# Moving the first third of the second layer's modulation product from between the layers to ahead of the first layer's routing

## The chip, the core and the metric

The kernel is one program on one core of a Trainium2 chip. TensorE does the matrix products, VectorE, ScalarE and GpSimd the rest; SyncE starts most of the transfers. The metric is the device time of one execution in microseconds (us), less being better. Times of day in this text are us from the start of the profiled execution's span.

## The reference

A block of two layers works on 256 latent and 256 context tokens of width 1024. Each layer modulates and normalizes the stream, mixes tokens, and adds a mixture of 16 experts, of which each token uses two. Cut to what matters here:

```
for layer in range(2):
    mod_l = cond_lat @ ada_w[layer] + ada_b[layer]          # ada_w: [2, 1024, 6144]
    mod_c = cond_ctx @ ada_w[layer] + ada_b[layer]
    sh1, sc1, g1, sh2, sc2, g2 = split(mod, 6)               # for latent and for context tokens
    n = rms_norm(h, norm_mix_g[layer]) * (1 + sc1) + sh1
    m = mixer(n)                                             # layer 0: convolution and scan; layer 1: convolution and attention
    h = h + g1 * (m @ w_out[layer])
    h = h + moe(rms_norm(h, norm_ffn_g[layer]) * (1 + sc2) + sh2)
out = rms_norm(h_lat, final_g)

def moe(t):
    score = sigmoid(t @ router_w)
    sel = (score + router_bias).reshape(-1, 4, 4)            # best group by its two best experts,
    ...                                                      # then the two best experts in it
    for e in range(16):
        out += combine[:, e] * ((silu(t @ w_gate[e]) * (t @ w_up[e])) @ w_down[e])
```

The change is about the columns `sh1, sc1` of `mod` in layer 1: the first 2048 of the 6144 columns of `ada_w[1]`, 8 MB. They depend on the conditioning vector alone, so they can be worked out at any time before the second layer's first normalization.

## The kernel before

**Precision.** Weights are split into a high half (`hi`, cast on ScalarE, L138) and the rest (`lo`, subtracted on VectorE, L140), and each product is three fast matmuls of halves. Such a pair of tiles is called `hl`. The modulation matrix is not split: it is multiplied as plain float32.

**The weight ring.** One object, `feed`, reads weight units of 1 MB ([128, 2048] float32) by transfers started from SyncE's queue into a ring of buffers: 3 called `raw`, 7 `rawx`, and 1 `rawy` that comes with the experts. `feed.one()` splits half a unit; after the second half of a unit `feed.load()` starts the next load into a buffer that is free. A load into a buffer whose splits aren't done waits on SyncE, and all that stands behind it in SyncE's program waits too. Before the experts, `moe()` sets `feed.gate = one`: the scale of the `hi` casts is then the tile `one`, which VectorE writes at the end of the routing (L1196), so that the splits of the first expert's weights come behind the routing.

**Layer 0, in order of time.** Output projection of the mixer (L788); routing; experts; the second layer's normalization `norm_T(1)` (L472 to L490); projections of the second mixer (L456). Tokens are in four tiles of 128.

**Routing.** Four tiles `H` give logits (L839) and, on VectorE and GpSimd, the normalized tokens `xn` (`normed`, L854 to L861), which SyncE writes to the DRAM table `XN` in four transfers of 512 KB (L861). `route()` ranks the scores on VectorE (L1082, then L998 to L1097), TensorE counts with a triangular matrix (`tri`, L1101), and VectorE makes the lists `dispi` (L1133), with which GpSimd gathers the first expert's tokens from `XN` into `xg` (L1134). `xg` is zeroed before on ScalarE (L1169). TensorE turns `xg` (L1150) and the first expert starts (L1162). Between routing and experts each engine reads the largest load `cnti` and jumps over a branch (L1007, L1008) that handles experts with over 128 tokens and isn't taken here.

**The moved product.** `Ada(1, 0)` covers the 2048 columns in eight units of 1 MB, each 256 columns wide, in rows of 1 KB (`ada_unit`, L330). One step (`channel_vectors`) is 8 float32 matmuls (L428), a copy on ScalarE (L430), and `channel_finish`: 2 small matmuls (L437) and one or two additions on VectorE (L441, L445) into the vectors `SH` and `SC`. In the kernel before, steps are made two at a time ahead of the columns k = 0, 2, 4, 6 of `norm_T(1)`, whose own work is 4 float32 matmuls for each k (L480), scale and shift by `SC`, `SH` on VectorE (L485) and ScalarE (L487), and a split (L489, L490). The loads are started in the tail of layer 0, three of them beside the reads of the experts' sums `YD`.

**What sets the order.** A scheduler at build time puts the instructions of each engine in one fixed row; the rows shown below under the change are read from the built programs. Engines run their rows in that order and wait by semaphores.

Of the kernel before, what the change touches and what calls it, by code (L numbers as in the profile page):

```python
# [17 lines left out]
NE = 16  # L18
# [29 lines left out]
HOLD = 0  # L48
ADA_PRE = 3
# [13 lines left out]
class Feeder:  # L63


    def __init__(self, tc, pool):
        self.tc, self.nc, self.pool = tc, tc.nc, pool
        self.boost = BOOST
        self.todo, self.loaded, self.ready = deque(), deque(), deque()
        self.extra, self.n, self.ahead, self.only = None, 0, 3, False  # L70
        self.gate = self.extra2 = self.hl = None
        self.np, self.part = 0, []
        self.ada, self.na, self.ns, self.pool_lo = None, 0, 0, 0

    def add(self, src, inner, columns=False):

# [19 lines left out]

    def load(self, n=99):
        limit = self.slots() if self.extra else 2
        while self.todo and len(self.loaded) < limit and n:
            n -= 1  # L100
            src, inner, columns = self.todo.popleft()
            t = self.raw_tile(True)
            if self.gate is not None:
                self.nc.vector.tensor_copy(t[:, 0:1], self.last)
            dst = t.rearrange("p (k f) -> p k f", f=inner)
            if callable(src):
                src = src()
            if type(src) is tuple:
                for i, part in enumerate(src):
                    self.nc.sync.dma_start(dst[:, :, 128 * i:128 * i + 128], part)  # L110
            else:
                self.nc.sync.dma_start(dst, src)
            self.loaded.append((t, columns))
# [55 lines left out]
def _body(tc, nc, pool, psum, dram, a):  # L169
# [39 lines left out]
    feed = Feeder(tc, pool)  # L209
# [297 lines left out]
    cmL, PL = open_pool("mix0_left")  # L507
# [234 lines left out]
    def add_experts(layer, u0, u1):  # L742
        parts = [("up", 0)]
        for e in range(NE):
            parts += [("gate", e)] + [("up", e + 1)] * (e + 1 < NE) + [("down", e)]
        us = []
        for part, e in parts:
            w = a["moe_w_" + part][layer, e].rearrange("(p k) f -> p k f", p=128)
            step = 2 if part == "down" else 4
            us += [(w[:, k0:k0 + step], 2048 // step) for k0 in (0, step)]  # L750
        for u in us[u0:u1]:
            feed.add(*u)
# [60 lines left out]
    ada_fill(40)  # L813
    feed.ada = None
    close_pool(cmR)
    add_experts(0, 0, 6 * NE - HOLD)
    cmX, PX = open_pool("raw0", "right")
    feed.extra, feed.n = (PX, RAWB0), -1
    feed.pool_lo = 0
# [249 lines left out]
    def route(layer, nt):  # L1069

        n_ = nt

        def xsteps(n):
            for st in XSTEPS[nt][n].split():
                normed(layer, int(st[0]), int(st[1]))

        xsteps(0)
        ins = S.activation(score[:, :nt], selt[:, :nt], AF.Sigmoid)
        mark("router", ins)
        dump(f"score{layer}", score)  # L1080
        se, sc = selt[:, :n_], score[:, :n_]
        V.tensor_tensor(se, sc, RB.unsqueeze(1).broadcast_to([128, n_, NE]), OP.add)  # L1082
        se4 = se.rearrange("p t (g e) -> p (t g) e", g=4)
        rk = rank[:, :n_]
        rk4 = rk.rearrange("p t (g e) -> p (t g) e", g=4)
        ranks(rk4, se4, 4 * n_)
        mk = mask[:, :n_]
        mk4 = mk.rearrange("p t (g e) -> p (t g) e", g=4)
        V.tensor_scalar(mk, rk, 1.5, None, OP.is_lt)
        xsteps(1)  # L1090
        pt_ = posm[:, :n_]
        V.tensor_tensor(pt_, mk, se, OP.mult)
        V.tensor_reduce(gsc[:, :n_].rearrange("p t g -> p (t g)"), pt_.rearrange("p t (g e) -> p (t g) e", g=4), AX.X, OP.add)
        ranks(grk[:, :n_], gsc[:, :n_], n_)
        V.tensor_scalar(grk[:, :n_], grk[:, :n_], 0.5, None, OP.is_lt)
        V.tensor_tensor(mk4, mk4, grk[:, :n_].rearrange("p t g -> p (t g)").unsqueeze(2).broadcast_to([128, 4 * n_, 4]), OP.mult)
        V.tensor_copy(maskb[:, :n_], mk)  # L1097

        pp_ = bank()
        for i in range(n_):  # L1100
            T.matmul(pp_[:, NE * i:NE * i + NE], tri, maskb[:, i], start=True, stop=i == 0)  # L1101
            for i2 in range(i):
                T.matmul(pp_[:, NE * i:NE * i + NE], oneb, maskb[:, i2], start=False, stop=i2 == i - 1)

        V.tensor_scalar(rk, rk, 0.5, pcol[:, 1:2], OP.is_gt, OP.add)
        if layer == 0:
            V.tensor_copy(RM[:, :n_, :, 0], rk)
        V.tensor_scalar(mk, mk, -16384.0, 16384.0, OP.mult, OP.add)
        V.tensor_tensor(posm[:, :n_], mk, pp_[:, :NE * n_].rearrange("p (t e) -> p t e", t=n_), OP.add)
        return xsteps, se, sc, mk, rk  # L1110

    def moe(layer, nt, pl, before_tail=None):
        A = Am[layer]
        n_ = nt
        xgs = [pl.tile([128, D], F32, name="xg", tag="xg", bufs=2) for _ in range(2)]

        xsteps, se, sc, mk, rk = route(layer, nt)

        def slots(e):
# [181 lines left out]
        with in_order():  # L1301
            expert(NE - 2)
            yss = [feed.raw_tile(True) for _ in range(nt)]
            for i in range(nt):
                Q.dma_start(yss[i], YD[256 * i:256 * i + 256].rearrange("(p t) d -> p (t d)", t=2))
            if before_tail:
                before_tail()
            for r in range(nt // 2):
                for nh in range(2):
                    S.activation(gbs[r][:, 512 * nh:512 * nh + 512], row_bc(A, 2, 2, r, nh), AF.Copy)  # L1310

            def add(i, st):
                ys = yss[i]
                if st == 0:
                    G.tensor_tensor(ys[:, :D], ys[:, :D], ys[:, D:], OP.add)
                elif st == 1:
                    V.tensor_tensor(ys[:, :D], ys[:, :D], gbs[i // 2], OP.mult)
                else:
                    V.tensor_tensor(Hi(i), Hi(i), ys[:, :D], OP.add)

            for i in range(nt):
                add(i, 0)
            for i in range(nt):
                for st in (1, 2):
                    later.append(lambda i=i, st=st: add(i, st))
            expert(NE - 1)
# [405 lines left out]
        for h in range(2):  # L1732
            feed.add(cdw[:, :, col0 + 256 * h:col0 + 256 * h + 256], 256, True)

    ada10 = Ada(1, 0)

    def prepare_mixer1():
        feed.only = True
        ada10.load(ADA_PRE)
        feed.only = False  # L1740

    def mixer1_weights():
        cblk(2048)
        cblk(1536)
# [6 lines left out]
                feed.add(w1[:, 4 * kh:4 * kh + 4, 512 * nh:512 * nh + 512], 512)  # L1751

    cmL, PL = open_pool("moe0")
    moe(0, 4, PL, prepare_mixer1)
    close_pool(cmL)
    close_pool(cmY)
    feed.extra2 = None
    feed.only = True
    ada10.load(3 - len(ada10.q))
    dump_h("H0")  # L1760
    if dbg.get("stop") == 1:
        return
# [2 lines left out]
    pend.extend(Ada(l, t) for l, t in ((0, 1), (0, 2), (1, 0), (1, 1), (1, 2))[3:])  # L1765
    cmM, PM = open_pool("mix1_m")
    cmL, PL = open_pool("mix1_n")
    nT = norm_T(1, PL, ada10)
    feed.extra, feed.only = None, False
    mixer1_weights()  # L1770
    feed.load()
    close_pool(cmX)
# [239 lines left out]
```

## Time and profile before

| what | value |
|---|---|
| median of 3 runs | 1205.16 us (1202.92 to 1210.82) |
| the profiled execution | 1208.15 us, its span 1206.5 us |
[...]
| TensorE busy | 1074.3 us, 89% |
| VectorE busy | 857.6 us, 71% |
| ScalarE busy | 716.6 us, 59% |
| GpSimd busy | 274.2 us, 23% |
| moved by DMA | 320.91 MB, mean 266 GB/s |

The profiled execution took 2.99 us more than the median, and 1.65 us of it lie outside its span. TensorE is the engine with the most work, so time is to be won where it stands still. The two stretches that the change touches are short: the routing of layer 0 (about 278 to 302) and the step from layer 0 to layer 1 (about 626 to 663).

### The profile page before, as it was taken

The page shows a single profiled execution, that of the slowest core. Times are in us where ns is not written, and L with a number is a line of the kernel's source. Part 1 is how long each engine was busy: PE and PEld are TensorE (multiplying, and loading weights), DVE is VectorE, ACT ScalarE, POOL GpSimd, SP SyncE. Part 2 cuts the span into 40 slices and gives each one's busy share as a digit, 9 for nine tenths or more (in the row PEclk, how much of TensorE's full clock was granted, in tenths as well). Part 3 has the DMA queues.
Part 4 walks back from the last instruction along what each step waited for, and adds up shares of the span by engine and source line. Part 5 has one row for each costly group of instructions (what it writes and reads, how often), then busy time and mean ns, then how long its engine had stood idle before and what let it go on. Part 6 is the DMA issues. An engine that isn't in the chain of part 4 may idle for free. (4 is left out here: it accounts for less than half of the span.)

```text
span 1206.5 us, 15581 instructions
## 1 busy us (share of the span) xinstructions
PE 1074.3 (89%) x5411; PEld 790.2 (65%) x5412; DVE 857.6 (71%) x1166; ACT 716.6 (59%) x971; POOL 274.2 (23%) x365
## 2 busy tenths in 40 slices
PE   4889999994999999999877899989499999999973
PEld 3556454783778787777666666657277777777762
DVE  2443571747888989989986144684888888798895
ACT  3326741533878788888726233452478788788861
POOL 3150461624011111112415400012301111110221
PEclk9989999997999999999988999999699999899986
DMA  9763757912899999999765766846379999899940
GB/s 299 222 206 92 219 175 243 378 42 92 332 353 358 337 355 366 362 368 352 290 201 175 230 222 250 299 172 244 114 276 352 343 376 366 318 374 355 337 163 35
DMA packets 101680, 320.91 MB, mean 266 GB/s; under 512 B 19040, under 2 KB 60147, under 8 KB 71896
## 3 DMA queue, kind: packets, MB, share of 16 engines
q1 hardware_dynamic: 90440, 298.63, 68.5%
q0 software_dynamic: 11152, 21.20, 5.5%
q8 instruction: 45, 0.74, 0.2%
q14 instruction: 43, 0.35, 0.1%
HBM read 308.58 MB, written 23.13 MB: 275 GB/s over the span
## 5 line engine op out<-in xcount | busy, mean ns | idle before, releaser
L140 DVE TENSOR_TENSOR hl<-rawx,hl 128x1024 fp32r<-128x1024 f32 x268 | 329.5, 1264 | 49.1 <-ACT hl L138 40.0
L138 ACT ACTIVATE hl<-rawx 128x1024 fp32r<-128x1024 f32 x260 | 268.5, 1058 | 61.5 <-PE psb L1566 15.2
L140 DVE TENSOR_TENSOR hl<-raw,hl 128x1024 fp32r<-128x1024 f32 x156 | 190.4, 1250 | 121.7 <-ACT hl L138 98.6
L138 ACT ACTIVATE hl<-raw 128x1024 fp32r<-128x1024 f32 x156 | 160.9, 1056 | 128.5 <-PE psa L456 41.5
L1162 PE MATMUL psb<-hl,xT 128*128 128x512 f32 x696 | 172.8, 401 | 0.0
L1566 PE MATMUL psb<-hl,xT 128*128 128x512 f32 x456 | 147.0, 426 | 15.8 <-DVE xT L1627 7.9
L1162 PEld LDWEIGHTS psb<-hl,xT 128*128 128x128 f32 x696 | 128.2, 189 | 27.6
L1566 PE MATMUL psa<-hl,xT 128*128 128x512 f32 x408 | 133.2, 424 | 2.1 <-DVE hl L140 1.7
L1566 PEld LDWEIGHTS psb<-hl,xT 128*128 128x128 f32 x456 | 89.7, 202 | 43.6 <-DVE xT L1627 9.0
L1566 PEld LDWEIGHTS psa<-hl,xT 128*128 128x128 f32 x408 | 80.3, 202 | 24.7 <-DVE hl L140 5.8
L1259 PE MATMUL psa<-hl,xT 128*128 128x512 f32 x192 | 77.9, 406 | 2.0 <-DVE hl L140 1.4
L1259 PE MATMUL psb<-hl,xT 128*128 128x512 f32 x192 | 77.9, 406 | 0.1
L456 PE MATMUL psa<-nT,hl 128*128 128x512 f32 x264 | 69.0, 405 | 4.7 <-POOL nT L490 2.5
L456 PEld LDWEIGHTS psa<-nT,hl 128*128 128x128 f32 x264 | 48.1, 188 | 28.5 <-issue 6.9
L456 PE MATMUL psb<-nT,hl 128*128 128x512 f32 x216 | 58.8, 419 | 4.5 <-DVE hl L140 2.6
L456 PEld LDWEIGHTS psb<-nT,hl 128*128 128x128 f32 x216 | 41.8, 198 | 21.4 <-issue 5.1
L1134 POOL DMA_INDIRECT xg<-XN,dispi x16 | 22.0, 1377 | 142.9 <-PE psb L1162 75.5
L1459 POOL DMA_INDIRECT YL<-y,dispi x14 | 15.4, 1100 | 154.4 <-ACT y L1645 152.1
L622 POOL DMA_DIRECT2D cz<-ups x64 | 35.0, 553 | 56.3 <-DVE th L689 41.6
L1259 PEld LDWEIGHTS psa<-hl,xT 128*128 128x128 f32 x192 | 37.2, 194 | 11.3 <-DVE hl L140 1.8
L1259 PEld LDWEIGHTS psb<-hl,xT 128*128 128x128 f32 x192 | 37.1, 193 | 10.5 <-DVE xT L1246 1.8
L1439 POOL DMA_INDIRECT xg<-XN,gidx x10 | 23.6, 2358 | 80.8 <-DVE gidx L1438 69.6
(539 smaller groups left out, 1815.4 us busy)
## 6 DMA issues: line engine op xcount, KB each, us to landing
rawx<-in_moe_w_up_dram SPq DMA_DIRECT2D x46, 1024.0 KB
rawx<-in_moe_w_gate_dram SPq DMA_DIRECT2D x44, 1024.0 KB
rawx<-in_moe_w_down_dram SPq DMA_DIRECT2D x42, 1024.0 KB
raw<-in_ada_w_dram SPq DMA_DIRECT2D x32, 1024.0 KB
raw<-in_moe_w_down_dram SPq DMA_DIRECT2D x20, 1024.0 KB
raw<-in_moe_w_gate_dram SPq DMA_DIRECT2D x17, 1024.0 KB
rawx<-in_ada_w_dram SPq DMA_DIRECT2D x16, 1024.0 KB
raw<-in_moe_w_up_dram SPq DMA_DIRECT2D x15, 1024.0 KB
```

What stands on the lines that cost most here:

```text
L138: nc.scalar.activation(h3, src, AF.Copy, scale=1.0 if self.gate is None else self.gate)
L140: (nc.gpsimd if self.pool_lo and self.ns % self.pool_lo == 0 else nc.vector).tensor_tensor(l3, src, h3.bitcast(F32), OP.subtract)
L456: ins = T.matmul(pt, l, r, start=k == 0 and m == 0, stop=k == 7 and m == 2)
L622: G.dma_start(z[32 * j:32 * j + 32, G4, :, :284], ups_[g][32 * G4:32 * G4 + 32, :, j:j + 284])
L1134: G.indirect_dma_start(out=xgs[e % 2], out_offset=None, in_=XN, in_offset=bass.IndirectOffsetOnAxis(ap=dispi[:, e, 1:2], axis=0), bounds_c ...
L1162: ins = T.matmul(out_, l, r_, start=m == 0, stop=m == last)
L1259: T.matmul(pb, l, w_[:, 512 * nh:512 * nh + 512], start=m == 0, stop=m == 11)
L1439: G.indirect_dma_start(out=xgs[n % 2], out_offset=None, in_=XN, in_offset=bass.IndirectOffsetOnAxis(ap=gidx[:, n:n + 1], axis=0), bounds_c ...
L1459: G.indirect_dma_start(out=YL, out_offset=bass.IndirectOffsetOnAxis(ap=dispi[:, j, 0:1], axis=0), in_=y, in_offset=None, bounds_check=1023 ...
L1566: ins = T.matmul(po, l, w_[:, c0:c0 + 512], start=k == 0 and m == 0, stop=k == 4 * per - 1 and m == len(mm) - 1)
```

## The change

The eight loads of `Ada(1, 0)` go into the weight ring behind the first expert's first two units, its `up` weights, so they are read long before the routing. `held` counts ring buffers that such a unit occupies. In `moe()`, ahead of `route()`, the eight steps are made; each gives its buffer back and lets the ring load one more expert unit. The steps and loads at the step between the layers go away, and `norm_T(1)` is built without them.

```
     def load(self, n=99):
         limit = self.slots() if self.extra else 2
-        while self.todo and len(self.loaded) < limit and n:
+        while self.todo and len(self.loaded) + self.held < limit and n:
             n -= 1
             src, inner, columns = self.todo.popleft()
+            if inner is None:
+                src()
+                self.held += 1
+                continue
...
-    add_experts(0, 0, 6 * NE - HOLD)
+    ada10 = Ada(1, 0)
+    add_experts(0, 0, 2)
+    for _ in range(8):
+        feed.add(ada10.load, None)
+    add_experts(0, 2, 6 * NE)
...
-    def moe(layer, nt, pl, before_tail=None):
+    def moe(layer, nt, pl):
...
+        for _ in range(8):
+            ada10.step()
+            feed.held -= 1
+            feed.load()
         xsteps, se, sc, mk, rk = route(layer, nt)
...
-            if before_tail:
-                before_tail()
...
-    ada10 = Ada(1, 0)
-
-    def prepare_mixer1():
-        feed.only = True
-        ada10.load(ADA_PRE)
-        feed.only = False
...
-    moe(0, 4, PL, prepare_mixer1)
+    moe(0, 4, PL)
...
-    feed.only = True
-    ada10.load(3 - len(ada10.q))
...
-    nT = norm_T(1, PL, ada10)
-    feed.extra, feed.only = None, False
+    nT = norm_T(1, PL)
+    feed.extra = None
```

The rows that follow are the fixed order of the built programs, an engine's instructions from top to bottom: line, operation, tiles, shape, how many. The changed kernel's lines have other numbers: L434, L436, L443, L447, L451 are L428, L430, L437, L441, L445 of the kernel before; L118 is L112, L144 is L138, L868 is L857, L872 is L861, L1009 to L1011 are L998 to L1000, L1018 is L1007, L1295 is L1279, L414 is L408, L493 and L495 are L487 and L489.

SyncE around the writes of `XN`, in the kernel before:

```order
L112 DMA rawx<-in_moe_w_up_dram 128x2048 x2
L112 DMA raw<-in_moe_w_down_dram 128x2048
L112 DMA raw<-in_moe_w_gate_dram 128x2048
L112 DMA rawx<-in_moe_w_gate_dram 128x2048
L861 DMA XN<-xn_1705 128x1024 x2
L861 DMA XN<-xn_1704 128x1024 x2
L1007 TENSOR_LOAD cnti
L1007 ISA x2
```

and in the changed one:

```order
L118 DMA rawx<-in_moe_w_gate_dram 128x2048
L872 DMA XN<-xn_1705 128x1024 x2
L118 DMA rawx<-in_moe_w_up_dram 128x2048 x2
L118 DMA rawx<-in_moe_w_down_dram 128x2048 x2
L118 DMA raw<-in_moe_w_up_dram 128x2048
L118 DMA rawx<-in_moe_w_gate_dram 128x2048 x2
L872 DMA XN<-xn_1704 128x1024 x2
L1018 TENSOR_LOAD cnti
L1018 ISA x2
L118 DMA raw<-in_moe_w_up_dram 128x2048
```

Before, the four writes stand together behind the ring's last load. Now the eight loads that follow the eight steps stand among them. Six of these take buffers that the moved product gives back; the last two `rawx` loads are given the buffers of the first expert's two `up` units, so each waits until VectorE has split that unit (L140), and those splits are gated by `one`. The second pair of writes stands behind these two.

VectorE ahead of the ranking (L998, changed L1009), before:

```order
L1082 TENSOR_TENSOR selt<-score,RB 128x64
L857 SCALAR_TENSOR_TENSOR xn_1704<-H,rs,psa 128x512 x2
L998 TENSOR_TENSOR tmp<-selt 128x256
L1000 TENSOR_TENSOR tmp<-selt 128x256
L999 TENSOR_TENSOR tmp<-tmp,lowm 128x256
L857 SCALAR_TENSOR_TENSOR xn_1704<-H,rs,psa 128x512
```

and the rows in the changed kernel from the last quarter of the moved product on:

```order
L447 TENSOR_TENSOR SH_109<-psa,PRT 128x4
L868 SCALAR_TENSOR_TENSOR xn_1704<-H,rs,psa 128x512
L447 TENSOR_TENSOR SC_107<-psb,PRT 128x4
L868 SCALAR_TENSOR_TENSOR xn_1704<-H,rs,psa 128x512
L451 SCALAR_TENSOR_TENSOR SC_107<-SC_107,PRT 128x4
L1009 TENSOR_TENSOR tmp<-selt 128x256
L1011 TENSOR_TENSOR tmp<-selt 128x256
L1010 TENSOR_TENSOR tmp<-tmp,lowm 128x256
```

All twelve additions of the product stand between the sum of score and bias (L1082, changed L1093) and the first comparison of the ranking. On TensorE the 64 matmuls L434 and the 16 matmuls L443 stand in one piece ahead of the first `tri` row, behind the last logits.

ScalarE where layer 0 ends, before:

```order
L1279 ACTIVATE yt<-psa,disp 128x512
L1279 ACTIVATE yt<-psb,disp 128x512
L408 ACTIVATE tmp,ss<-H 128x512 x5
L138 ACTIVATE hl<-raw 128x1024
L408 ACTIVATE tmp,ss<-H 128x512
L138 ACTIVATE hl<-raw 128x1024
L408 ACTIVATE tmp,ss<-H 128x512
L430 COPY tmp<-psa 128x256
L408 ACTIVATE tmp,ss<-H 128x512
L430 COPY tmp<-psb 128x256
L138 ACTIVATE hl<-raw 128x1024
```

and in the changed kernel:

```order
L1295 ACTIVATE yt<-psa,disp 128x512
L1295 ACTIVATE yt<-psb,disp 128x512
L144 ACTIVATE hl<-raw 128x1024 x2
L414 ACTIVATE tmp,ss<-H 128x512 x8
L493 ACTIVATE tmp<-psa,SH_109,SC_107 128x256
L493 ACTIVATE tmp<-psb,SH_109,SC_107 128x256
L495 ACTIVATE nT<-tmp 128x512 x2
L493 ACTIVATE tmp<-psa,SH_109,SC_107 128x256
L493 ACTIVATE tmp<-psb,SH_109,SC_107 128x256
L495 ACTIVATE nT<-tmp 128x512 x2
```

The eight sums of squares (L408, changed L414) stand together now, without two casts of projection weights and two copies of the product among them.

Two more moves stand in these orders: the zeroing of `xg` (L1169) and the first two gathers (L1134), which came ahead of the jump L1008, come behind it, and four gated casts stand ahead of it on ScalarE where there were two.

## Rows read from the trace of the kernel before

**Rows 1.** Work by stretch: window, its length, busy us of each engine, clock, DMA share, GB/s.

```profile
core 0: us, PE busy (x) PEld busy (x) DVE busy (x) ACT busy (x) POOL busy (x), PEclk, DMA share, GB/s
248.00:302.00 54.00, 38.23 (x227) 30.09 (x225) 33.43 (x76) 20.20 (x38) 18.54 (x23) 0.85 0.15 53
302.00:587.00 285.00, 275.57 (x1298) 220.33 (x1298) 254.55 (x296) 231.26 (x267) 37.53 (x33) 0.99 0.93 345
634.00:663.00 29.00, 22.02 (x227) 17.50 (x227) 17.26 (x36) 17.84 (x41) 15.47 (x19) 0.88 0.56 182
```

**Rows 2.** The same view, shorter stretches: ring loads, routing, normalization.

```profile
220.00:240.00 20.00, 19.79 (x93) 15.98 (x93) 15.11 (x23) 9.60 (x12) 13.36 (x8) 1.00 1.02 421
276.00:283.00 7.00, 6.97 (x28) 3.85 (x28) 4.57 (x9) 1.45 (x3) 4.32 (x5) 1.00 0.09 37
642.00:648.00 6.00, 5.87 (x32) 5.46 (x36) 4.03 (x9) 3.48 (x8) 2.11 (x4) 0.51 1.10 349
```

**Rows 3.** Order of time on VectorE, routing: start, duration, operation, idle time before.

```profile
281.76 1.26 DVE L998 TENSOR_TENSOR tmp<-selt 128x256 f32<-128x256 f32 x1
285.75 0.73 DVE L857 SCALAR_TENSOR_TENSOR xn<-H,rs,psa 128x512 f32<-128x512 f32 x1
294.49 0.15 DVE L1196 TENSOR_SCALAR one<-disp 128x1 f32<-128x1 f32 x1
296.03 1.23 DVE L140 TENSOR_TENSOR hl<-rawx,hl 128x1024 fp32r<-128x1024 f32 x1
```

**Rows 4.** The same for TensorE.

```profile
278.43 1.10 PE L733 MATMUL psb<-Am,ident 128*128 128x512 f32 x2
291.43 0.20 PE L1101 MATMUL psa<-maskb,tri 128*128 128x16 bf16 x2 [8.46 <-DVE maskb L1097]
300.16 1.09 PE L1150 MATMUL psa<-ident,xg 128*128 128x128 f32 x4 [4.24 <-DMA xg<-XN,dispi]
```

**Rows 5.** The same for ScalarE and GpSimd.

```profile
283.58 1.99 ACT L1169 ACTIVATE xg<-score 128x1024 f32<-128x1024 f32 x2
294.67 2.19 ACT L138 ACTIVATE hl<-rawx,one 128x1024 fp32r<-128x1024 f32 x2 [9.09 <-DVE one L1196]
294.62 1.20 POOL L1134 DMA_INDIRECT xg<-XN,dispi  x1 [5.45 <-DVE cnt L1189]
```

**Rows 6.** The tile XN, 270 to 310, and SyncE's waits, 240 to 302.

```profile
L861 SPq DMA_DIRECT2D XN<-xn x4: 319/320/333, 281.5 to 289.2; - x4
DMA to landing us min/median/max: 5.3/5.5/5.7
SPq L112 <- DVE hl L140: 11.2, 1, 11.2
```

**Rows 7.** Order of time on TensorE, normalization of layer 1.

```profile
642.13 1.02 PE L437 MATMUL psa<-gsum,tmp 128*128 128x2 f32 x4 [6.25 <-ACT tmp L430]
647.55 1.21 PE L428 MATMUL psa<-rawx,condT 128*32 128x256 f32 x16
648.59 1.04 PE L428 MATMUL psb<-rawx,condT 128*32 128x256 f32 x16
649.56 0.61 PE L437 MATMUL psa<-gsum,tmp 128*128 128x2 f32 x4
650.02 1.14 PE L480 MATMUL psa<-tmp,H 128*128 128x128 f32 x8
662.53 5.83 PE L456 MATMUL psa<-nT,hl 128*128 128x512 f32 x24
```

**Rows 8.** ScalarE and VectorE in the same stretch.

```profile
638.61 1.04 ACT L138 ACTIVATE hl<-raw 128x1024 fp32r<-128x1024 f32 x1
641.73 0.35 ACT L430 COPY tmp<-psa 128x256 f32<-128x256 f32 x1
644.77 0.29 DVE L472 TENSOR_SCALAR tmp<-ident,rs 128x128 f32<-128x128 f32 x1 [0.93 <-POOL rs L412]
```

**Rows 9.** VectorE's last sum of layer 0, and TensorE's next wait behind the normalization.

```profile
636.24 1.04 DVE L1346 TENSOR_TENSOR H<-H,tmp 128x512 f32<-128x512 f32 x1
678.61 1.94 PE L353 MATMUL psb<-raw,condT 128*32 128x512 f32 x8 [3.46 <-DMA raw<-in_ada_w_dram]
```

More of the change, by code (lines that the diff above doesn't have):

```diff
@@ L73, in __init__ @@
         self.ada, self.na, self.ns, self.pool_lo = None, 0, 0, 0
+        self.held = 0
     def add(self, src, inner, columns=False):
```

## The prediction

> **What bounds the kernel now.** I read the work by stretch first [rows 1]: it tells which engine stands still where. In the experts, 302 to 587, TensorE is busy 275.57 of 285 us; what the change does to loads there can hardly win anything. In the routing, 248 to 302, TensorE is busy 38.23 of 54 us and the DMA share is 0.15, and between the layers, 634 to 663, it is busy 22.02 of 29 us. These two stretches have room, and the change takes work out of the second and puts it into the first. So the question is what ends last in each.
>
> For the routing I read each engine in order of time. VectorE's first comparison starts at 281.76 and `one`, the end of the routing, is written at 294.49: a chain of 12.73 us that VectorE works on nearly without a gap [rows 3]. TensorE has done its last product for the tokens at 278.43 + 1.10 = 279.5 and waits 8.46 us for that chain, then 4.24 us for the gathered tokens, and starts the first expert with L1150 at 300.16 [rows 4]. The gather was issued at 294.62 [rows 5] and takes 5.3 to 5.7 us to land [rows 6]. So the path is VectorE's chain, then the gather; what TensorE has to spare, it has only while VectorE's chain runs.
>
> **Part 1: the steps ahead of the ranking.** The two matmul groups of a pair of steps start at 647.55, 648.59, and the L437 behind them at 649.56, with the next work at 650.02 [rows 7]. That is 1.0 us for each L428 group and 0.46 us for each L437: 2.9 us for a pair, 11.7 us for the four pairs. By full durations instead (1.04 and 0.61) it is 3.3 and 13.2 us. [...] The block begins at 279.5 and ends at about 291.5 to 293. If TensorE's idle time alone counted, it would be free: 8.46 us of waiting and 4.24 us more stand there. But VectorE's row has all twelve additions of the product in front of the first comparison, and the last addition needs the last L437. Behind it VectorE has at most a token product of 0.73 us [rows 3] before the comparison. So the chain starts at 293 to 294.5 and not at 281.76: it is 11.5 to 13 us later; I take 12. `one` comes at 306.5.
>
> [...]
>
> **Part 2: the writes of XN.** Before, the last write of `XN` was issued at 289.2 [rows 6], ahead of the gather's lists, so the gather waited for the lists alone. Now the second pair of writes stands on SyncE behind two loads that wait for gated splits. After `one` (306.5) VectorE's first gated split starts 296.03 - 294.49 = 1.54 us later, and four of 1.23 us follow [rows 3]; ScalarE's four casts, 1.1 us each [rows 5], keep ahead of it. The first `up` unit is split at about 310.5, the second at 313. The second load is issued then, and the two writes behind it at about 313.3. A 1 MB load takes 2.5 us at the 421 GB/s of the ring loads [rows 2]; the two writes of 512 KB take as much again. They land at about 318 if the load goes first. Such waits of SyncE for a split exist before as well, 11.2 us of one load in this stretch [rows 6], but nothing that the routing needed stood behind it.
>
> [...]
>
> The gather then starts at 318 and lands 5.5 us later, up to 2.5 us later still with the next 1 MB load beside it, so L1150 starts at 324 to 326.5 in place of 300.16: I take 25 us. The zeroing of `xg` (1.99 us, [rows 5]) now stands behind the jump on ScalarE, but it would end by about 315, ahead of the writes. The bounds of this term: 12 us, if the gather follows the routing chain alone, and 29 us, if the second load is late by a split more and the gather shares the queues with three loads.
>
> While TensorE waits, the DMA queues load what the ring has room for, as before. The experts start with a full ring in both kernels, and they are bound by TensorE [rows 1], so nothing is given back there: 0 (bounds 0 and -2).
>
> **Part 3: what is taken out between the layers.** In the normalization TensorE does eight groups L428, eight L437 and the L480; L456 starts at 662.53 [rows 7]. Statistics first: ScalarE's sums of squares lose two casts of 1.04 us and one copy of 0.35 us from among them [rows 8], so the last diagonal (644.77) comes 2 to 2.5 us earlier, at about 642.5. From there the loop over k has only L480, two groups of 1.14 us for a pair of k at the upper clock [rows 7], the first ones near double that since the clock was 0.51 in 642 to 648 [rows 2]. VectorE and ScalarE need about 2.5 us for a pair of k as well. Four pairs take some 10 us in place of 18, so L456 starts at about 653: 9.5 us earlier. Against it stands that the second projection unit is now split on VectorE between the last sums of layer 0 (two of 1.2 us, ahead of the L1346 that ends at 637.3 [rows 9]), which can cost up to 3 us; for it speaks that the wait of 3.46 us for an `ada_w` unit at 678.61 [rows 9] may go. I leave these two against each other and take -9.5 us, bounds -6 and -13.
>
> **Sum.** 25 - 9.5 = +15.5 us on the profiled execution's 1208.15 us gives 1223.7 us. The median stands 2.99 us below that execution, so I expect a median of 1221 us. Bounds: 12 - 13 = -1 us, or 1204 us, and 29 - 6 = +23 us, or 1228 us.
>
> **The rivals.**
> First, nothing much: the gather isn't held by the writes, because the splits and loads are through before the lists are, or the writes are small beside the loads. Then the loss is the chain's 12 us, perhaps 15 with the zeroing behind the jump, and the gain 9.5 to 13: -1 to +5.5 us, a median of 1204 to 1211 us. For it: SyncE's queue was never late for the routing so far. Against it: the order itself, in which those writes stand behind splits that can't begin before `one`.
> Second, faster: the product is hidden in TensorE's standstill. That is so if the ranking starts at its old time, which needs VectorE to have the last additions behind the comparisons, or the product done by 282. Price: the gain of part 3 without a loss, -9.5 to -13 us, a median of 1192 to 1196 us. The point that decides is the start of the first comparison: at or before 284 this rival holds. For it: 12.7 us of TensorE's waiting stand there. Against it: the product alone takes 11.7 us from 279.5, and VectorE's row.
> Third, worse: the gains are eaten where they arise, because VectorE's split of the second projection unit stands in the last sums and waits for a load that is late. Then part 3 gives 4 us or less and the sum is +21 to +27 us, a median of 1226 to 1232 us. For it: that load takes the buffer of the first projection unit, which must be split first.
>
> **How the numbers follow.** My forecast (1213 to 1226 us) gets 0.55, the first rival 0.28, the second 0.05, the third 0.12. The range of 8 in 10 takes in the first rival and reaches into the third: 1204 to 1230 us; outside are the second rival and the upper part of the third, with some 0.05 for a term that I don't see. A change of this kernel under 1%, 12 us, can't be told from none with certainty. Over 1% slower is above 1217.2 us: four fifths of the forecast (0.44) and the third rival (0.12) make 0.56. Faster by over 1% is below 1193.1 us: half of the second rival, and a little for the unseen, 0.04. That leaves 0.40.
>
> **What would show it.** In the changed kernel's trace: 64 L434 and 16 L443 in one piece from about 279.5 to 292; the first comparison (L1009) at 293 to 294.5; `one` at about 306.5; SyncE's last write of `XN` at about 313, behind two loads; the gather landing at 322 or later and L1150 at 324 to 326.5, with TensorE standing still for nearly all of the time from 293. Experts as long as before, 285 us. Between the end of VectorE's last L1346 (637.28) and the first L456 some 16 us in place of 25.25. I am wrong in part 2 if the last write of `XN` is issued before 308 or the gather waits for its lists alone; in part 1 if the first comparison is ahead of 290; in part 3 if the normalization is bound by ScalarE or by projection weights and not by the removed steps.

## The result and the profile after

The changed kernel takes 1221.74 us, median of 5 runs (1220.5 to 1227.03), against 1206.73 us of 5 runs before: ratio 1.0132 with a 95% interval of 1.0102 to 1.0163, 15.0 us slower by the medians. Its profiled execution took 1227.03 us, the longest of its five, with a span of 1225.3 us. Against the profiled execution before (1208.15 us) that is +18.9 us.

**Where it went, by stretch.** Four landmarks cut both spans: the first matmul on the gathered tokens, the first matmul of layer 0's sums over experts (L1342, now L1356), VectorE's last sum (L1346, now L1360), and the first projection matmul of layer 1 (L456, now L462).

| stretch | before, us | after, us | difference, us |
|---|---|---|---|
| start to first matmul on `xg` | 300.16 | 333.08 | +32.9 |
| to the first L1356 | 326.15 | 327.94 | +1.8 |
| to the end of VectorE's last L1360 | 10.97 | 15.48 | +4.5 |
| to the first L462 | 25.25 | 10.66 | -14.6 |
| to the end | 543.97 | 538.14 | -5.8 |

So the normalization gives back 14.6 us, 10.1 of them net of the longer last sums, and the routing costs 32.9, some three times the net. The windows of the changed kernel's trace answer to [rows 1, 2]; the columns are the same, the clock being the share of TensorE's full speed that was granted.

```profile
276.00:283.00 7.00, 7.00 (x39) 5.18 (x36) 3.03 (x7) 1.12 (x3) 3.37 (x5) 0.76 0.00 0
316.00:328.00 12.00, 0.00 (x0) 0.00 (x0) 1.72 (x4) 3.24 (x3) 0.00 (x0) 0.50 0.97 337
328.00:330.00 2.00, 0.00 (x0) 0.00 (x0) 0.00 (x0) 0.00 (x0) 1.20 (x1) 0.50 0.23 94
335.00:620.00 285.00, 275.22 (x1294) 220.30 (x1294) 252.19 (x293) 229.89 (x265) 37.25 (x33) 0.99 0.91 338
677.00:688.00 11.00, 10.14 (x68) 10.02 (x69) 5.17 (x11) 7.09 (x19) 5.15 (x12) 0.76 0.00 1
```

The experts are bound by TensorE as before (275.22 us busy of 285). From 316 to 328 no matmul runs at all, while the DMA queues move 337 GB/s: 4.05 MB in 12 us. That is the standstill to be explained. TensorE in order of time, answering to [rows 4, 7]:

```profile
281.18 2.05 PE L739 MATMUL psb<-Am,ident 128*128 128x512 f32 x2
283.17 1.94 PE L434 MATMUL psa<-rawx,condT 128*32 128x256 f32 x16
290.08 0.61 PE L443 MATMUL psa<-gsum,tmp 128*128 128x2 f32 x4
293.56 0.61 PE L443 MATMUL psa<-gsum,tmp 128*128 128x2 f32 x4
308.27 0.22 PE L1112 MATMUL psa<-maskb,tri 128*128 128x16 bf16 x2 [6.63 <-DVE maskb L1108]
333.08 1.09 PE L1166 MATMUL psa<-ident,xg 128*128 128x128 f32 x4 [20.32 <-DMA xg<-XN,dispi]
```

A pair of steps takes 293.56 - 290.08 = 3.48 us here. The wait in front of the first expert has grown from 4.24 to 20.32 us, and it is for the gather. VectorE, answering to [rows 3]:

```profile
298.65 0.75 DVE L868 SCALAR_TENSOR_TENSOR xn<-H,rs,psa 128x512 f32<-128x512 f32 x1 [0.80 <-PE psa L739]
300.12 0.42 DVE L1009 TENSOR_TENSOR tmp<-selt 128x256 f32<-128x256 f32 x1
311.34 0.14 DVE L1212 TENSOR_SCALAR one<-disp 128x1 f32<-128x1 f32 x1
```

The first comparison starts behind the product, at 300.12 in place of 281.76. SyncE and GpSimd between them show what the gather waited for: three rows of SyncE, the gather, and SyncE's waits from 300 to 322 [rows 5, 6]:

```profile
315.26 2.66 SPq L118 DMA_DIRECT2D rawx<-in_moe_w_gate_dram  x2
318.01 0.86 SPq L872 DMA_DIRECT2D XN<-xn  x2
319.79 0.34 SPq L118 DMA_DIRECT2D raw<-in_moe_w_up_dram  x1
...
328.51 1.20 POOL L1150 DMA_INDIRECT xg<-XN,dispi  x1 [22.49 <-issue]
...
SPq L118 <- DVE hl L146: 17.2, 1, 17.2
```

SyncE stands 17.2 us in front of a load whose buffer VectorE must split first; the writes of `XN` follow at 318.01, and GpSimd issues the gather only at 328.51, though its lists were there at about 311. The row names no releaser ("issue"), but the trace records when each transfer landed: the two loads in front of the writes at 320.22 and 324.82, the writes at 325.98 and 327.22, 1.3 us ahead of the gather. GpSimd's waits for these two in front of L1150 end at 326.00 and 327.24.

At the other end, VectorE's last sums and TensorE behind them [rows 7, 9]:

```profile
665.15 0.68 DVE L1359 TENSOR_TENSOR tmp<-psa,gb 128x512 f32<-128x512 f32 x1
666.17 3.25 DVE L146 TENSOR_TENSOR hl<-raw,hl 128x1024 fp32r<-128x1024 f32 x2 [0.34 <-ACT hl L144]
669.35 0.68 DVE L1359 TENSOR_TENSOR tmp<-psb,gb 128x512 f32<-128x512 f32 x1
675.46 1.04 DVE L1360 TENSOR_TENSOR H<-H,tmp 128x512 f32<-128x512 f32 x1
681.29 0.28 DVE L478 TENSOR_SCALAR tmp<-ident,rs 128x128 f32<-128x128 f32 x1 [0.78 <-POOL rs L418]
```

```profile
677.86 0.80 PE L486 MATMUL psa<-tmp,H 128*128 128x128 f32 x2 [9.36 <-DVE tmp L478]
...
687.16 3.26 PE L462 MATMUL psa<-nT,hl 128*128 128x512 f32 x13
701.56 1.06 PE L359 MATMUL psb<-raw,condT 128*32 128x512 f32 x8
```

Two splits of projection weights stand between the first sum and the second, as feared. TensorE's 64 matmuls of the normalization (L486) start 1.4 us after the last sum and run without the product from 677.86 to 687.16, while the diagonals (L478) are still being made. The wait of 3.46 us at L353 (now L359) is gone.

### The profile page after: what moved, and what is told of

The parts are those of the page before. It is cut to its first block, busy times and chain, and to the rows that moved or that the text cites. A ratio compares the mean times of both kernels' runs of the same rounds, so it can differ in the third digit from the quotient of the medians.

```text
span 1225.3 us, 15579 instructions
## 1 busy us (share of the span) xinstructions
PE 1079.9 (88%) x5411; PEld 794.9 (65%) x5412; DVE 851.7 (70%) x1165; ACT 716.9 (59%) x971; POOL 272.9 (22%) x365
## 5 line engine op out<-in xcount | busy, mean ns | idle before, releaser
L144 ACT ACTIVATE hl<-rawx 128x1024 fp32r<-128x1024 f32 x260 | 268.9, 1059 | 62.8 <-PE psb L1580 15.8
L146 DVE TENSOR_TENSOR hl<-raw,hl 128x1024 fp32r<-128x1024 f32 x154 | 186.1, 1237 | 125.5 <-ACT hl L144 103.0
L144 ACT ACTIVATE hl<-raw 128x1024 fp32r<-128x1024 f32 x154 | 158.9, 1057 | 132.5 <-PE psa L462 41.4
L462 PE MATMUL psa<-nT,hl 128*128 128x512 f32 x264 | 70.2, 409 | 6.1 <-POOL nT L496 3.7
L462 PEld LDWEIGHTS psa<-nT,hl 128*128 128x128 f32 x264 | 48.3, 189 | 30.5 <-issue 6.9
L462 PE MATMUL psb<-nT,hl 128*128 128x512 f32 x216 | 59.4, 421 | 4.3 <-DVE hl L146 2.6
L1150 POOL DMA_INDIRECT xg<-XN,dispi x16 | 21.4, 1339 | 159.6 <-PE psa L1260 75.3
L462 PEld LDWEIGHTS psb<-nT,hl 128*128 128x128 f32 x216 | 42.1, 199 | 20.3 <-issue 3.8
```

Of the source, the lines that this page charges most:

```text
L144: nc.scalar.activation(h3, src, AF.Copy, scale=1.0 if self.gate is None else self.gate)
L146: (nc.gpsimd if self.pool_lo and self.ns % self.pool_lo == 0 else nc.vector).tensor_tensor(l3, src, h3.bitcast(F32), OP.subtract)
L462: ins = T.matmul(pt, l, r, start=k == 0 and m == 0, stop=k == 7 and m == 2)
L1150: G.indirect_dma_start(out=xgs[e % 2], out_offset=None, in_=XN, in_offset=bass.IndirectOffsetOnAxis(ap=dispi[:, e, 1:2], axis=0), bounds_c ...
```

## The experiments

The theory: the loss is the sum of two waits in a row, the ranking behind the product and the gather behind the writes of `XN`; the gain is the shorter normalization. The rivals: the lower clock level seen at the start of the block (0.50 in 280 to 286), a loss in the experts from a ring that refills late, the zeroing of `xg` behind the jump. e1, e2, e3 and e5 ran on one chip with 29 runs of the kernel before (median 1207.45 us), e4, e6, e8 and e9 on another with 18 (median 1210.18 us), and the change beside the 5 runs named above; so the ratios are compared, not the times.

| kernel | median, us | ratio to before | 95% interval |
|---|---|---|---|
| the change | 1221.74 | 1.0132 | 1.0102 to 1.0163 |
| e1_no_product | 1197.67 | 0.9903 | 0.9873 to 0.9933 |
| e2_two_loads_later | 1214.11 | 1.0061 | 1.0034 to 1.0088 |
| e3_zero_first | 1209.95 | 1.0007 | 0.9979 to 1.0035 |
| e5_matmuls_in_gap | 1203.50 | 0.9952 | 0.9925 to 0.9979 |
| e6_sums_first | 1219.09 | 1.0068 | 1.0044 to 1.0093 |
| e4_after_ranking | 1209.82 | 1.0001 | 0.9973 to 1.0029 |
| e8_gap_loads_later | 1201.71 | 0.9906 | 0.9872 to 0.9940 |
| e9_gap_loads_sums | 1204.75 | 0.9937 | 0.9906 to 0.9968 |

**e1: the gain by itself.** The product is left out of both places.

```
-    for _ in range(8):
-        feed.add(ada10.load, None)
+    V.memset(SCs[1], 1.0)
+    V.memset(SHs[1], 0.0)
...
-        for _ in range(8):
-            ada10.step()
-            feed.held -= 1
-            feed.load()
```

> The changed kernel without the moved product at all: its eight loads and eight steps are left out, SC and SH of layer 1 are set to constants. This is the gain between the layers without any price. Theory (gain about 10 us between the layers, loss about 25 us at the routing): 1194 to 1198 us, L1166 of the first expert at about 300 as before the change. Rival (little is won between the layers, since the last sums of layer 0 are held up by a split and TensorE starts the normalization at half clock): 1202 to 1206 us.

The ratio 0.9903 is -11.7 us of 1207.45. The routing is back at its old times, VectorE's first comparison and TensorE's first work for an expert:

```profile
282.12 1.26 DVE L1009 TENSOR_TENSOR tmp<-selt 128x256 f32<-128x256 f32 x1
...
300.72 1.09 PE L1162 MATMUL psa<-ident,xg 128*128 128x128 f32 x4 [4.44 <-PEq L1019]
```

So -11.7 us is the whole of what there was to win with the product gone, and the change lost some 27 us in the routing (1.0132 - 0.9903 = 2.3%). The last sums are long here as well, 16.51 us from their first matmul to the last sum, with two splits of projection weights ahead of the sums and not among them; so their length doesn't come from the product, and what else sets it stays open. That the bracket names the sequencer (PEq, line 1019) shows that the jump, and not the gather, ended TensorE's wait here, 4.44 us after its last counting matmul; the gather had landed 0.9 us earlier (299.87).

**e2: the writes of XN ahead of the gated loads.** The two loads that wait for gated splits are started behind the writes.

```
-        for _ in range(8):
+        for i in range(8):
             ada10.step()
             feed.held -= 1
-            feed.load()
+            if i < 6:
+                feed.load()
...
         xsteps(2)
+        feed.load()
```

> The changed kernel with the last two of the eight loads started behind the writes of XN in place of ahead of them. Theory (those writes were held behind gated loads): the last write of XN is issued at about 306 to 309, as soon as the tokens are ready; the gather then waits for the zeroing of xg, which ScalarE does behind the gated casts, until about 317; the first transposes (L1168 or so) at 322 to 324 in place of 333, and 1211 to 1213 us. Rival (TensorE's 14 to 16 us of product are the loss, and the writes only wait beside it): no change, 1220 to 1223 us.

1.0061: some 8.6 us of the loss come back (1.0132 - 1.0061 = 0.71%). The first transposes stand at 322.25, as expected; the median is 1 us above the expected 1213. The last write of `XN` is now started at 301.6, but GpSimd waits for another thing, and its gather is slow; GpSimd in order of time, and the tile `xg`, from issue to landing:

```profile
312.56 1.56 POOL L1152 DMA_INDIRECT xg<-XN,dispi  x1 [10.99 <-ACT xg L1187]
...
DMA to landing us min/median/max: 9.5/10.8/12.1
```

The zeroing on ScalarE (L1187), which the prediction had called harmless because the writes come later, became the last wait once the writes were early: it stands behind the jump and four gated casts. And the gather takes 9.5 to 12.1 us beside four loads of 1 MB that SyncE started between 310.81 and 313.46, where [rows 6] had 5.3 to 5.7.

**e3: the zeroing out of the way as well.** As e2, with GpSimd zeroing `xg`.

```
-            S.activation(t, score[:, 0, 0:1].broadcast_to([128, D]), AF.Copy, scale=0.0)
+            G.memset(t, 0.0)
```

> As the one with the two loads later, and xg is zeroed by GpSimd's memset ahead of the gathers in place of by ScalarE behind the gated casts. Theory: the gather follows the lists alone, at about 311 to 312, the first transposes at about 317, and 1205 to 1208 us: what is left of the loss is the ranking's delay of 15 to 18 us against 10 us won. Rival (the zeroing has no part in it): the same as without it.

1.0007 (0.9979 to 1.0035): no difference from before; the median of 1209.95 is 2 us above the expected range. The gather now follows the lists alone:

```profile
309.86 1.20 POOL L1151 DMA_INDIRECT xg<-XN,dispi  x1 [5.15 <-DVE cnt L1207]
...
DMA to landing us min/median/max: 4.5/5.4/6.4
...
315.62 1.09 PE L1167 MATMUL psa<-ident,xg 128*128 128x128 f32 x4 [4.46 <-PEq L1019]
```

This splits the loss. Between the change and e3 lie 1.25%, 15 us: what the gather waited for beyond its lists. Between e3 and e1 lie 1.04%, 12.6 us: the product in front of the ranking, with its eight loads in the ring, which e1 leaves out too. In the traces the first work for an expert stands at 300.72 (e1), 315.62 (e3) and 333.08 (the change).

**e4: the steps behind the ranking.**

```
-        for _ in range(8):
-            ada10.step()
...
         xsteps, se, sc, mk, rk = route(layer, nt)
+        for _ in range(8):
+            ada10.step()
```

> The changed kernel with one edit: the eight steps with their loads are written behind the routing's ranking in place of ahead of it, whole, each with its small matmuls and additions. In the built order two groups of matmuls stand ahead of the tri matmuls and six behind, and VectorE's additions are spread through the later part of the routing. Theory (the ranking's delay on VectorE and the held-up writes are the loss): the first comparison at 282 to 283, the gather 4 to 8 us later than before the change, the first transposes at 306 to 312, and 1203 to 1210 us. Rival (the loss is TensorE's work wherever it stands): 1215 us or more.

1.0001: no difference from before, and against the rival. The first comparison is back at 284.54, but the first transposes come at 316.71 and not at 306 to 312: the product comes among the counting and spreads through the routing at the lower clock (0.50 from 290 to 306), 1.93 us a group of 16 matmuls:

```profile
297.51 1.93 PE L434 MATMUL psa<-rawx,condT 128*32 128x256 f32 x16
...
310.00 0.59 PE L443 MATMUL psa<-gsum,tmp 128*128 128x2 f32 x4
316.71 1.09 PE L1166 MATMUL psa<-ident,xg 128*128 128x128 f32 x4 [5.93 <-PEq L1019]
```

The order of the steps in the program is not enough: TensorE's part has to go into the standstill, and VectorE's part out of the chain.

**e5: only the 64 large matmuls in the standstill.** `route()` calls them behind the comparisons; the 16 small matmuls and the additions come behind the lists. The results of the large ones wait in tiles of their own.

```
+        def matmuls():
+            A0s.extend(pl.tile([128, D], F32, name="A0", tag="y", bufs=3) for _ in range(2))
+            for i in range(8):
+                fins.append(channel_vectors(1, ada10.q.popleft(), i, A0s[i // 4][:, 256 * (i % 4):256 * (i % 4) + 256]))
+                ada10.k += 1
+                feed.held -= 1
+                feed.load()
+        xsteps, se, sc, mk, rk = route(layer, nt, matmuls)
...
+        for fin in fins:
+            fin()
         overflow(layer, nt, pl, posm, YD)
```

> The changed kernel with the product cut in two: the eight groups of matmuls and their copies run in TensorE's standstill during the ranking, and the small matmuls and VectorE's additions come behind the lists of the gather; the writes of XN come ahead of all loads but one. Theory (the loss is VectorE's row and SyncE's row, not TensorE's work): ranking and gather at their old times, the first transposes at 300 to 304, and 1195 to 1200 us, faster than both kernels. Rival (TensorE's work is the loss, and it shifts the first expert by its length wherever it stands): at least 8 us above the kernel without the product, 1204 us or more.

0.9952 (0.9925 to 0.9979): faster than before. At 1203.50 us, 5.8 us above e1, it lies between the theory (1195 to 1200) and the rival (1204 or more). The eight groups run from 283.91 to 291.02, 1.05 to 1.07 us each (1.07 and 1.05 in e6 at a clock of 1.00, 1.93 in e4 at 0.50), with nothing waiting for them. What is lost now:

```profile
302.95 0.99 PE L443 MATMUL psb<-gsum,A 128*128 128x2 f32 x4
307.17 1.09 PE L1173 MATMUL psa<-ident,xg 128*128 128x128 f32 x4 [3.23 <-DMA xg<-XN,dispi]
...
DMA to landing us min/median/max: 9.3/10.1/10.9
```

The gather was issued at 297.73, but takes 9.3 to 10.9 us beside the five loads that SyncE had started from 290.69 to 294.5. It landed at 307.03; TensorE's jump, which took 6.04 us here (the row gives ns), was through at 306.6, so a faster gather alone would have won at most 0.4 us:

```profile
L1019 PEldq COMPARE_BRANCH  x1: 6037/6037/6037, 300.6 to 300.6; - x1
```

**e6: the last sums first.** The change as it is, with the projection weights' splits at a lower priority in the scheduler until the first projection.

```
     feed.extra = None
+    feed.boost = 100
     mixer1_weights()
...
         S.copy(kT[:, 512 * g:512 * g + 512], proj(nT, feed.get()))
+        feed.boost = BOOST
```

> The changed kernel with the splits of the second projection unit at a lower place in the scheduler's order, so that they come behind nearly all of layer 0's last sums in place of ahead of them. Theory (these splits hold up the sums by about 4 us, which the normalization then lacks): VectorE's last sum (L1360) 3 to 4 us earlier against the last L1356, and 1217 to 1220 us. Rival (the projection's weights are needed as early as that, so that the 4 us come back as a wait of TensorE for them): 1221 to 1223 us.

1.0068 against 1.0132 of the change: from the first L1356 to the last sum it takes 12.10 us in place of 15.48. That is 3.4 us of the 7.7 between the ratios; where the rest comes from isn't shown. This run is also the fairest look at the routing, whose order is that of the change, since the clock was at its upper level when the block began (1.00 in 276 to 283; a group of 16 took 1.07 us, not 1.94). VectorE's first comparison, the tile `XN`, GpSimd and TensorE:

```profile
294.84 0.41 DVE L1009 TENSOR_TENSOR tmp<-selt 128x256 f32<-128x256 f32 x1
...
L872 SPq DMA_DIRECT2D XN<-xn x4: 319/364/383, 281.5 to 313.2; - x4
...
323.51 1.20 POOL L1150 DMA_INDIRECT xg<-XN,dispi  x1 [22.77 <-issue]
...
328.30 1.09 PE L1166 MATMUL psa<-ident,xg 128*128 128x128 f32 x4 [20.83 <-DMA xg<-XN,dispi]
```

```profile
311.00:323.00 12.00, 0.00 (x0) 0.00 (x0) 1.43 (x4) 2.97 (x3) 0.00 (x0) 0.50 0.94 339
```

The last write is started at 313.2 and the gather at 323.51, after 12 us with 339 GB/s (4.07 MB). By the trace's record of landings the two loads ahead of the writes, started at 309.97 and 312.30, landed at 314.95 and 319.79, the writes at 320.97 and 322.21, and the load started behind them only at 324.65.

**e8: as e5, with loads and small matmuls later.** Only three loads ahead of the gather, the rest behind it; the small matmuls behind the jump.

```
-                feed.load()
+                if i < 3:
+                    feed.load()
...
-        for fin in fins:
-            fin()
         overflow(layer, nt, pl, posm, YD)
         feed.gate, feed.boost = one, GBOOST
+        feed.load()
         feed.split()
+        for fin in fins:
+            fin()
```

> The kernel with the matmuls in the gap, with two things moved: five of the eight loads that refill the ring come behind the jump, and the small matmuls and VectorE's additions come behind the jump too. Theory (the gather took 9.3 to 10.9 us in place of 5.5 because the ring's loads shared the queues with it, and the additions held up the tile one): the gather lands in 6 to 8 us, the first transposes at 302 to 304 in place of 307.2, and 1197 to 1201 us. Rival (the experts need these loads early, so that TensorE waits for weights in the first experts): 1203 us or more, with waits for hl on TensorE between 310 and 350.

0.9906 (0.9872 to 0.9940): faster than both kernels, and as far below the kernel before as e1, which leaves the product out. The gather takes 6.6 us with three loads started ahead of it (291.56 to 292.86) in place of five. The first work for an expert is nevertheless later than in e5, and not at 302 to 304 as expected: TensorE's jump still takes 5.75 us, and the small matmuls now stand between the jump and that work, at the lower clock (0.50 in 301 to 312; 0.85 us apart):

```profile
304.60 0.98 PE L443 MATMUL psa<-gsum,A 128*128 128x2 f32 x4 [7.01 <-PEq L1019]
...
310.56 0.99 PE L443 MATMUL psb<-gsum,A 128*128 128x2 f32 x4
311.42 1.09 PE L1174 MATMUL psa<-ident,xg 128*128 128x128 f32 x4
```

At the start of the experts e5 is ahead (307.17 against 311.42), but its experts take 332.3 us where those of e8 take 328.04, and the ratios' intervals overlap. So that e8 is better than e5 isn't shown.

**e9: e8 with e6's edit.** It should add up.

> Both of the former: matmuls in the gap, loads and additions behind the jump, splits of the second projection unit behind the sums. Theory: the sum of both, 1194 to 1198 us. Rival (either gain is eaten by waits for weights): 1200 us or more.

0.9937 (0.9906 to 0.9968), not better than e8; the intervals overlap. The median of 1204.75 us is on the rival's side. The last sums take 12.11 us in place of 13.47, and the experts 331.19 in place of 328.04 in the profiled pair. Whether the edit is worth anything there stays open.

## Why the prediction was right

The forecast was 1221 us, the median is 1221.74, and the mechanism is the forecast's: ranking behind the product, gather behind the writes of `XN`, a shorter normalization. That the size came out within 1 us is in part luck. In the traces the routing lost more than forecast (28 to 33 us, not 25), and more came back behind it (10.1 us between the layers and 5.8 in the rest, not 9.5 in all), so that the errors partly cancel.

- **Part 1, the chain behind the product.** Right. `one` at 306.5 was forecast; it stood at 306.05 in e6 and at 311.34 in the change's own profiled execution, which had the clock at its lower level for the last logits and the first groups (0.76 in 276 to 283, 0.50 in 280 to 286) and began the block at 283.17, not 279.5 (279.46 in e6). The pair's price was too small: 3.48 us, not 2.9 to 3.3, as the small matmuls L443 and the next step's first rows take turns (L443 at 290.08, two of L434 at 290.62, L443 at 291.17, L434 at 291.71), 0.54 us from one to the next where the forecast had 0.46 for each L437. One reading was wrong: TensorE's last product for the tokens ended at 282.97, not at 279.5, since four more pairs of L733 follow the one read; the 8.46 us of waiting count from there. In the change one of these pairs (now L739, at 297.51) runs between the last two groups L443, so the product is not quite in one piece and its end is 0.9 us later for it. VectorE's chain behind the block was in turn shorter, 11.2 us (294.84 to 306.05 in e6, 300.12 to 311.34) and not 12.73; its first comparison took 0.42 us where [rows 3] had 1.26. Before, it ran beside GpSimd's L858 (280.25 to 285.55); in the profiled execution of the change GpSimd's L869 begins at 300.69, and there the first two comparisons take 0.42 us and the third, begun at 300.79, takes 1.49. That GpSimd is the cause wasn't tested.
- **Part 2, the writes of XN.** Right in kind, wrong in size. Issue was forecast at 313.3, and e6 has 313.2 for the last one's start. Landing was forecast at 318, from 1 MB of load and 1 MB of writes at 421 GB/s; in e6 the last write landed at 322.21. The step that failed is the load's 2.5 us from its issue. The second load, started at 312.30, landed 7.5 us later, at 319.79; the first one, started at 309.97, had landed at 314.95, 5.0 us after its start. Behind the second load the writes took 2.4 us (2.5 forecast), and the gather followed 1.3 us later, at 323.51. The third load, behind the writes, landed after them (324.65). Why the second load needed 4.8 us behind the first isn't shown. That it was the writes the gather waited for is shown by their landings, and by e2, where GpSimd waits for the zeroing instead. Then the gather: 5.5 to 8 us forecast, 328.30 - 323.51 = 4.8 us to the transposes, with 53 GB/s moved from 323 to 325. Together L1150 (now L1166) comes at 328.3 in e6 and 333.08 in the profiled execution, against 324 to 326.5: this term is 28 to 33 us, not 25, and the 33 of the profiled execution lies outside the bounds of 12 and 29.
- **The cover of the zeroing.** Right as put: it ended at 313.98 in e6 and at 319.25 in the profiled execution (315 forecast), ahead of the landing of the writes. But e2 shows that it was only covered: with the writes early, the zeroing is next, and a gather beside loads after it.
- **Part 3, between the layers.** The sum was right, -10.1 us (+4.5 - 14.6) against -9.5, by two errors of opposite sign. The last sums, with the splits among them, took 4.5 us more, where "up to 3" was allowed; with the splits moved behind nearly all of them (e6) 3.4 of these come back. The normalization took 10.66 us from the last sum to the first L462, where the forecast had 15.7 (637.3 to 653). Its two parts had the right length: the last diagonal comes 4.8 us behind the last sum (681.29 - 676.50; 7.5 before), and the loop takes 9.3 us (some 10 forecast). But the forecast put the loop behind the last diagonal; it runs beside the diagonals, because the loop's first matmuls need the first diagonal alone (L478 from 677.52, L486 from 677.86), and nothing of the product stands ahead of them on TensorE any more. The third rival's mechanism is thus real, and was paid for by this.
- **Experts at nothing.** +1.8 us in the profiled pair. In e2, e3, e5 and e9 the stretch is 331 to 335 us, in all other kernels 324 to 328. I found no single wait of that size in their traces, so the cause stays open.
- **The rest**, 5.8 us less from the first L462 on, was not forecast but for the wait of 3.46 us at L353, which is gone; the other 2.3 us I can't place.

By medians: e1 gives -11.7 us, the product in front of the ranking +12.6, the writes with the zeroing and the loads beside the gather +15; the forecast had -9.5, +12 and +13. The three add up to the change's 1.32% by construction, since each is a difference between neighbours, so their sum is no check; each has an interval of some 0.3 to 0.4% to either side, 4 to 5 us.

The clock, a rival of the experiments, is not the loss: e6 had the upper level at the start of the block (1.00 in 276 to 283) and still stood at 328.30. The rival "faster" was wrong for this order, but its price was right for another one: with TensorE's matmuls in the standstill and VectorE's additions behind the lists (e8), the time is 0.94% below before, where 1192 to 1196 us, 1.1 to 0.8% below, had been named.

## What to carry to other kernels

An idle engine hides moved work only if the other engines' parts of it also miss the chain: the 8.46 us of TensorE's standstill were usable for the matmuls (e5, e8) and worthless for a product whose additions stood in front of the ranking. When a step is moved, follow each of its side effects down its own queue: here the buffers that it frees started loads, and two of those held up writes that the next stage reads. Take away waits one at a time and read what ends last each time; the order here was writes, zeroing, then the gather beside loads (landed at 307.03 in e5) and TensorE's jump (through at 306.6), which end nearly together.

## What the runs showed of the hardware

- The same gather of two blocks landed 4.5 to 6.4 us after issue where the transfers moved 14 to 207 GB/s (e3, 310 to 316) and 9.3 to 12.1 us beside four or five loads of 1 MB (e2, e5), about twice as long. It was not held behind those loads: in e5 its first part landed at 307.03 and the last of the loads, started earlier, at 309.98. The gather is issued by GpSimd, the loads by SyncE; the writes of `XN`, issued by SyncE as the loads are, did land behind the loads ahead of them (e6, below).
- In e6 the two writes landed 8.3 and 9.0 us after they were started, behind the two loads ahead of them and in front of the load behind (324.65). In e3, with no load started in the 7 us before, the same writes landed 2.6 and 2.7 us after their start, as all four did before the change (2.6 to 2.7 us, from 281.54 to 291.87).
- The jump L1019 took longest on TensorE. The first row is TensorE's in e1, the second TensorE's in e8, the third GpSimd's in e1 (ns):

```profile
L1019 PEldq COMPARE_BRANCH  x1: 3725/3725/3725, 296.5 to 296.5; - x1
L1019 PEldq COMPARE_BRANCH  x1: 5754/5754/5754, 298.5 to 298.5; - x1
L1019 POOLq COMPARE_BRANCH  x1: 57/57/57, 295.9 to 295.9; - x1
```

  It took 3.4 to 3.7 us before the change, in the change, e1, e2, e3 and e6, 4.33 in e4, and 5.65 to 6.04 in e5, e8 and e9, where the transfers moved 309 to 408 GB/s meanwhile, against 124 in e1, 121 before the change and 19 in the change. Within each of these jumps the trace has one packet of 16 KB of the kind "instruction": 297.87 to 298.84 in e1, 301.90 to 302.93 in e8, and likewise 297.22 to 298.26 before the change and 314.00 to 315.04 in the change. That TensorE waits for this packet isn't shown.
- TensorE's clock fell to its lower level just ahead of the block in one execution (1.00 in 276 to 278, 0.50 in 280 to 286 in the change) and stayed at the upper in another of the same order (1.00 in 276 to 283 in e6), though TensorE was busy without a gap from 270 on in both (7.00 of 7.00 us in 276 to 283). The block began 3.7 us later in the first (283.17 against 279.46); 2.0 of these stood before the clock fell (the same pair of L739 starts at 277.77 and 275.78).
